# A decoder layer on one core: block 1's products with the expert input table made dense, the output columns split 768/256

## The chip, the core and the metric

The kernel runs on one core of a Trainium2 chip. The metric is the device time of one execution in microseconds. Before the change three runs took 1105.27, 1107.07 and 1106.55 us, so the median is 1106.55 us.

## What is computed

One decoder layer on 256 tokens of width 1024: a mixer (sparse attention beside gated linear attention), a cross-attention to a fixed memory, and PEER, a retrieval among 128 x 128 experts of one neuron each, with a layer norm behind each. The change lies in PEER alone:

```python
# 8 heads; per head the 16 best of 128 x 128 pairs of sub-keys: experts (T, 128), gates (T, 128)
def block(args):                       # one block of 128 tokens
    xt, et, gt = args
    u = expert_down[et]                # input table: 16384 rows of 1024
    act = jax.nn.gelu(jnp.einsum('td,tkd->tk', xt, u), approximate=False)
    vv = expert_up[et]                 # output table: 16384 rows of 1024
    return jnp.einsum('tk,tkd->td', gt * act, vv)
```

Every token so takes 128 rows of each table. There are two blocks of 128 tokens, called block 0 and block 1.

## The kernel before

TensorE (PE), VectorE (DVE), ScalarE (ACT) and GpSimd (POOL) are fed by Python code which is unrolled into one program. The framework orders each engine's instructions by priority and simulated readiness, starting from the order in which the code writes them; SP (SyncE) issues the plain loads and POOL the gathers.

**Up to about 269 us** the mixer, the cross-attention's keys and block 0's attention run. The change doesn't touch them.

**Input rows, 269 to 785 us.** `pick` (L645) finds the best keys and experts of one or two heads on DVE: `best16` (L748) with MAX8, FIND_INDEX8 and MATCH_REPLACE8, then one-hot products. `query` (L899) loads 1 MB of query weights and makes a head's scores on PE. `down` (L915) handles one column of 128 experts at a time: POOL gathers 128 rows of 4 KB, one for each token (`gd`, five buffers, L924 to L926), and DVE multiplies them with the tokens and sums (`junk`, L927), which gives one column of `wt`. There are 128 such steps for block 0 and 128 for block 1. For block 1 the tokens are first rearranged: `spread` (L711) and `quarter_rows` (L935) put each token on four partitions, so that a gather serves 32 tokens with four experts each.

The loop at L1050 mixes picks, rows and, from its step 5, the scatter. **The scatter** turns the gated weights of a block into a matrix `W[b]` of all 16384 experts against 128 tokens: `second_keys` (L1005) writes one-hot columns of the second sub-key with five ACT instructions for four tokens, and `weights` (L1014) makes for each token a one-hot of the first sub-key times the weights on DVE (`oa`, L1036), a product on PE of the strided column `W[b][:, :, t]` with it (L1037, two matmul instructions, as for each fp32 product), and writes back four tokens at a time on ACT (L1041). Block 1's scatter (L1116 to L1145) follows each quarter of its rows.

**Output table, 777 to 1084 us.** `up_dense` (L1166) loads the output table row by row (`u`, 128 pieces of 512 KB), splits each into a high and a low part (`uh` on ACT L1178, `ul` on DVE L1179), splits `W` alike (`w`, L1172 and L1173), and multiplies: three terms, each of them 512 columns per matmul into `py`. Block 0 has all 1024 columns by matmul, block 1 only the first `CD` = 512; its other 512 come from `up_rows_dve` (L1100), which gathers half rows (`gu`, L945) and sums them on DVE (`yq`, L1109). That makes 9 matmuls of 512 columns for a table row. A layer norm and the stores end the kernel (L1202 to L1226).

Of the kernel before, what the change touches and what calls it, by code (L numbers as in the profile page):

```python
# [44 lines left out]
OA = 6  # L45
YQ = 1
# [37 lines left out]
def kernel(ctx: ExitStack, tc, I, out):  # L84
# [560 lines left out]
    def pick(b, h0, n):  # L645

        def heads(t):

            if b == 0:
                return t[:, h0 * 16:(h0 + n) * 16].rearrange("p (n r) -> p n r", n=n)  # L650
            return t.rearrange("p (m g r) -> p m g r", m=4, g=2)[:, h0 % 4:h0 % 4 + n, h0 // 4, :]

        sel = [heads(PK[b]["sel"][:, e, :]) for e in range(2)]
        if b == 0:
            ei, gt = heads(PK[0]["ei"]), heads(PK[0]["gt"])
        else:
            ei, gt = heads(eg[:, 0, :]), heads(eg[:, 1, :])
# [42 lines left out]
        vec.scalar_tensor_tensor(ei[:, :, rs], sel[0][:, :, rs], 128.0, sel[1][:, :, rs], op0=OP.mult, op1=OP.add)  # L700
# [7 lines left out]
        if b == 1 and h0 + n in (4, 8):  # L708
            spread(h0 // 4)

    def spread(g):  # L711


        p = smt("sp").rearrange("p (q e r) -> p q e r", q=16, e=2)
        for q in range(4):
            for m in range(4):
                pe.matmul(p[32 * m:32 * m + 32, q], lhsT=ident[:, 32 * q:32 * q + 32],
                          rhs=eg[:, :, 32 * m + 16 * g:32 * m + 16 * g + 16],
                          start=True, stop=True, tile_position=(0, 32 * m))
        for e, nm in enumerate(("ei", "gt")):  # L720
            vec.tensor_copy(PK[1][nm].rearrange("p (q r) -> p q r", q=4)[:, :, 16 * g:16 * g + 16], p[:, :4, e, :])
# [45 lines left out]
    def picked(b):  # L767
        pt = smt("tp")
        for e in range(2):
            pe.transpose(pt[:, e * 128:(e + 1) * 128], PK[b]["sel"][:, e, :], ident)  # L770
        ixT = PK[b]["ixT"] = keep.tile([128, 128], FT, tag="ixT", name="ixT")
        nix = PK[b]["nix"] = keep.tile([128, 128], FT, tag="nix", name="nix")
        act.copy(ixT, pt[:, 0:128])
        act.mul(nix, pt[:, 128:256], -1.0)  # L774
# [100 lines left out]
    eg = work.tile([128, 2, 128], FT, tag="sc", name="eg", bufs=2)  # L875
# [37 lines left out]
    junk = consts.tile([128, DM], BF, name="junk")  # L913

    def down(b, pieces, tokens):  # L915

        ei, wt, gt = [PK[b][k] for k in ("ei", "wt", "gt")]
        xs = {}
        for i, j in enumerate(pieces):
            for k in range(16 * j, 16 * j + 16):  # L920
                for q in {0: pieces[i:i + 1], QR: pieces[i + 1:i + 2]}.get(k % 16, ()):
                    if q // 2 not in xs:
                        xs[q // 2] = tokens(q // 2)
                g = gath.tile([128, DM], FT, tag="gd", name="gd")  # L924
                gp.indirect_dma_start(out=g, out_offset=None, in_=I["dn"],  # L925
                                      in_offset=bass.IndirectOffsetOnAxis(ap=ei[:, k:k + 1], axis=0))  # L926
                vec.tensor_tensor_reduce(out=junk, in0=g, in1=xs[j // 2], scale=1.0, scalar=0.0, op0=OP.mult,  # L927
                                         op1=OP.add, accum_out=wt[:, k:k + 1])
                if k % 16 == 15:
                    hs = slice(k - 15, k + 1)  # L930
                    act.activation(wt[:, hs], wt[:, hs], AF.Gelu)
                    vec.tensor_mul(wt[:, hs], wt[:, hs], gt[:, hs])
                yield

    def quarter_rows(q, pool, tag, bufs, fold):  # L935

        x = pool.tile([128, DM], FT, tag=tag, name="xq", bufs=bufs)
        rs = slice(32 * q, 32 * q + 32)
        for i in range(2):
            p, cs = smt("xq"), slice(512 * i, 512 * i + 512)  # L940
            pe.matmul(p, lhsT=fold[rs, :], rhs=H2[1][rs, cs], start=True, stop=True, tile_position=(32 * q, 0))
            act.copy(x[:, cs], p)
        return x

    def up_row(b, k, pool):  # L945
        g = pool.tile([128, CG], FT, tag="gu", name="gu")
# [21 lines left out]
    def rest(b):  # L968
# [8 lines left out]
        if b == 0:  # L977
# [4 lines left out]
        h2T[b] = slot("h2T", [128, 8, 128])  # L982
# [4 lines left out]
    fold = load(work, "fold", [128, 128], tag="k4")  # L987
    rows = itertools.chain(down(0, range(8), lambda q: H2[0]),
                           down(1, (0, 2)[:EARLY], lambda q: quarter_rows(q, work, "pp", 3, fold)))
# [15 lines left out]
    def second_keys(b, g):  # L1005

        nix = PK[b]["nix"]
        o = W[b][:, :, 4 * g:4 * g + 4]
        for j in range(4):
            t = 4 * g + j  # L1010
            act.activation(o[:, :, j], iot, AF.Abs, bias=nix[:, t:t + 1])  # L1011
        act.activation(o, o, AF.Relu, scale=-1.0, bias=1.0)

    def weights(b):  # L1014
# [3 lines left out]
        if b == 0:  # L1018
            pt = smt("tr")
            pe.transpose(pt[:, 0:128], PK[b]["wt"], ident)  # L1020
            vec.tensor_copy(wT, pt[:, 0:128])
        ps = {}
        for g in range(33):
            if b == 1 and g % 8 == 0 and g < 32:
                pt, qs = smt("tr"), slice(4 * g, 4 * g + 32)
                for m in range(4):
                    ms = slice(32 * m, 32 * m + 32)
                    pe.matmul(pt[ms, 0:32], lhsT=PK[1]["wt"][ms, qs], rhs=ident[ms, ms], start=True, stop=True,
                              tile_position=(32 * m, 32 * m))
                vec.tensor_copy(wT[:, qs], pt[:, 0:32])  # L1030
            if g < 32:
                ps[g] = smt("wb")
                for j in range(4):
                    t = 4 * g + j
                    a = sml.tile([128, 128], FT, tag="oa", name="oa", bufs=OA)
                    vec.tensor_scalar(a, iot, ixT[:, t:t + 1], wT[:, t:t + 1], op0=OP.is_equal, op1=OP.mult)  # L1036
                    pe.matmul(ps[g][:, j * 128:(j + 1) * 128], lhsT=W[b][:, :, t], rhs=a, start=True, stop=True)  # L1037
                    yield
            if g:
                t0 = 4 * (g - 1)  # L1040
                act.activation(W[b][:, :, t0:t0 + 4], ps[g - 1].rearrange("p (j i) -> p i j", j=4), AF.Copy)  # L1041

    todo = ((0, 1, 2), (0, 3, 2), (0, 5, 2), (0, 7, 1), (1, 0, 2), (1, 2, 2), (1, 4, 2), (1, 6, 2))
    both = HB + 1
    asked = {0: [(h, (0,)) for h in range(QF, 3)], 1: [(h, (0,) if h <= HB else B2) for h in (3, 4)],
             2: [(h, B2) for h in (5, 6, 7)], 3: [(h, (1,)) for h in (1, 2)],
             4: [(h, (1,)) for h in (3, 4) if h <= HB]}
    nd, nk, nw = 0, 0, 0
# [239 lines left out]
```

## Time and profile before

| | |
|---|---|
| median of three runs | 1106.55 us |
| the profiled execution, its own time | 1103.19 us |
| its span, first to last instruction | 1101.1 us |
| busy: PE, DVE, ACT, POOL | 801.6, 941.1, 517.8, 494.9 us |
| moved by DMA | 293.39 MB, mean 266 GB/s |

The page gives an engine's busy time as a share of the span. A busy PE is modelled from pipelined instructions, so matmuls are better counted by their starts. [...]

### The profile page before, as it was taken

How to read it: one execution, taken by the hardware profiler on the slowest of the kernel's cores; microseconds unless marked ns; L12 is line 12 of the kernel's file. 1: busy time of each engine (PE TensorE's matmuls, PEld its weight loads, DVE VectorE, ACT ScalarE, POOL GpSimd, SP SyncE). 2: the span in 40 equal slices, each digit the busy share in tenths (PEclk: the TensorE clock that was granted, in tenths of full speed). 3: DMA queues.
4: the chain of work that ended last, by engine and by line, in shares of the span. 5: the costliest groups of instructions: out<-in, count | busy, mean ns of one | idle time of the engine just before them, and what ended most of it. 6: DMA issues, size and time to landing. Idle time of an engine off the chain costs nothing. (4 is left out here: it accounts for less than half of the span.)

```text
span 1101.1 us, 13910 instructions
## 1 busy us (share of the span) xinstructions
PE 801.6 (73%) x4341; PEld 653.2 (59%) x4341; DVE 941.1 (85%) x2155; ACT 517.8 (47%) x983; POOL 494.9 (45%) x391
## 2 busy tenths in 40 slices
PE   7999998997658910010556866853799999999994
PEld 6998878987548800000344545643677677677772
DVE  6957877556877899999997999999799998899996
ACT  5557653451202211896124894211255556565661
POOL 0000000001555786567533768787265662476671
PEclk9999999898779965555555655655799999999997
DMA  8454224554989988888864888788589999899993
GB/s 299 158 189 171 98 96 173 178 185 143 337 286 377 335 300 317 314 300 283 273 210 131 320 283 302 257 308 303 222 304 352 342 355 325 288 353 364 356 358 115
DMA packets 76297, 293.39 MB, mean 266 GB/s; under 512 B 9520, under 2 KB 10304, under 8 KB 70208
## 3 DMA queue, kind: packets, MB, share of 16 engines
q0 software_dynamic: 47104, 167.80, 43.7%
q1 hardware_dynamic: 28832, 123.67, 31.6%
q10 hardware_dynamic: 288, 1.05, 0.3%
q8 instruction: 34, 0.56, 0.2%
q14 instruction: 39, 0.32, 0.1%
HBM read 291.43 MB, written 1.05 MB: 266 GB/s over the span
## 5 line engine op out<-in xcount | busy, mean ns | idle before, releaser
L925 POOL DMA_INDIRECT gd<-dn,ei x256 | 314.8, 1230 | 433.4 <-ACT s1b L897 267.8
L947 POOL DMA_INDIRECT gu<-upg,ei x128 | 175.3, 1369 | 149.0 <-DVE yq L1109 77.2
L76 PE MATMUL py<-uh,w 128*128 128x512 f32 x768 | 222.1, 396 | 20.9 <-ACT uh L1178 19.5
L76 PE MATMUL wb<-oa,W 128*128 128x128 f32 x512 | 148.9, 444 | 74.1 <-DVE oa L1036 73.0
L1178 ACT ACTIVATE uh<-u 128x1024 fp32r<-128x1024 f32 x128 | 135.7, 1060 | 116.0 <-PE py L76 80.8
L76 PEld LDWEIGHTS wb<-oa,W 128*128 128x128 f32 x512 | 120.0, 308 | 111.3 <-DVE oa L1036 71.9
L76 PEld LDWEIGHTS py<-uh,w 128*128 128x128 f32 x768 | 145.1, 190 | 56.8 <-ACT uh L1178 20.4
L927 DVE CUSTOM_DVE_ANT_0 junk<-gd,h 128x1024 bf16<-128x1024 f32 x128 | 155.3, 1213 | 17.4 <-DMA gd<-dn,ei 16.7
L927 DVE CUSTOM_DVE_ANT_0 junk<-gd,xq 128x1024 bf16<-128x1024 f32 x128 | 155.6, 1215 | 10.7 <-DMA gd<-dn,ei 10.5
L1179 DVE TENSOR_TENSOR ul<-u,uh 128x1024 fp32r<-128x1024 f32 x128 | 156.0, 1219 | 9.7 <-ACT uh L1178 9.0
L76 PE MATMUL py<-ul,w 128*128 128x512 f32 x384 | 139.8, 418 | 5.2 <-DVE ul L1179 4.9
L239 DVE TENSOR_TENSOR wlo<-w,whi 128x1024 fp32r<-128x1024 f32 (+1 forms) x68 | 81.3, 1196 | 46.9 <-PE mm L76 35.7
L1109 DVE SCALAR_TENSOR_TENSOR yq<-gu,wt,yq 128x512 f32<-128x512 f32 x124 | 93.0, 750 | 6.2 <-DMA gu<-upg,ei 5.4
L237 ACT ACTIVATE whi<-w 128x1024 fp32r<-128x1024 f32 (+1 forms) x68 | 70.5, 1039 | 53.4 <-PE mm L76 39.8
L1041 ACT ACTIVATE W<-wb 128x512 f32<-128x512 f32 x64 | 38.1, 597 | 113.3 <-PE wb L76 113.2
L76 PEld LDWEIGHTS py<-ul,w 128*128 128x128 f32 x384 | 64.8, 190 | 44.0 <-DVE ul L1179 34.3
L1011 ACT ACTIVATE W<-ii,nix 128x128 f32<-128x128 f32 x256 | 89.1, 491 | 0.4 <-ACT nix L774 0.4
L1036 DVE TENSOR_SCALAR oa<-ii,ixT,wT 128x128 f32<-128x128 f32 x256 | 80.1, 347 | 5.5 <-PE wb L76 2.2
L76 PE MATMUL mm<-whi,xPh 128*128 128x256 f32 (+1 forms) x176 | 50.9, 292 | 6.1 <-ACT xPh L246 6.1
L76 PE MATMUL mm<-h2T,w 128*128 128x128 f32 x448 | 52.3, 275 | 2.8 <-DMA w<-pq 2.8
L76 PE MATMUL mm<-wlo,xPh 128*128 128x256 f32 (+1 forms) x176 | 52.0, 296 | 1.6 <-DVE wlo L239 1.6
L76 PEld LDWEIGHTS mm<-h2T,w 128*128 128x128 f32 x448 | 51.1, 192 | 3.5 <-DMA w<-pq 3.4
(332 smaller groups left out, 1398.3 us busy)
## 6 DMA issues: line engine op xcount, KB each, us to landing
u<-upd SPq DMA_DIRECT2D x128, 512.0 KB, 6.0
w<-pq SPq DMA_DIRECT2D x10, 1024.0 KB, 5.0
w<-xo SPq DMA_DIRECT2D x8, 1024.0 KB, 4.8
w<-xk SPq DMA_DIRECT2D x4, 1024.0 KB, 6.0
w<-xv SPq DMA_DIRECT2D x4, 1024.0 KB, 4.8
w<-wo SPq DMA_DIRECT2D x4, 1024.0 KB, 4.8
w<-xq SPq DMA_DIRECT2D x4, 1024.0 KB, 4.8
gd<-dn,ei POOLq DMA_INDIRECT x256, 5.8
```

The costliest lines, as they stand in the source:

```text
L76: self.eng.matmul(out, lhsT=lhsT, rhs=rhs, **kw)
L237: act.activation(hi, src, AF.Copy)
L239: eng.tensor_sub(lo, src, hi.bitcast(FT))
L925: gp.indirect_dma_start(out=g, out_offset=None, in_=I["dn"], in_offset=bass.IndirectOffsetOnAxis(ap=ei[:, k:k + 1], axis=0))
L927: vec.tensor_tensor_reduce(out=junk, in0=g, in1=xs[j // 2], scale=1.0, scalar=0.0, op0=OP.mult, op1=OP.add, accum_out=wt[:, k:k + 1])
L947: gp.indirect_dma_start(out=g, out_offset=None, in_=I["upg"], in_offset=bass.IndirectOffsetOnAxis(ap=PK[b]["ei"][:, k:k + 1], axis=0))
L1011: act.activation(o[:, :, j], iot, AF.Abs, bias=nix[:, t:t + 1])
L1036: vec.tensor_scalar(a, iot, ixT[:, t:t + 1], wT[:, t:t + 1], op0=OP.is_equal, op1=OP.mult)
L1041: act.activation(W[b][:, :, t0:t0 + 4], ps[g - 1].rearrange("p (j i) -> p i j", j=4), AF.Copy)
L1109: vec.scalar_tensor_tensor(y, g, wt[:, k:k + 1], y, op0=OP.mult, op1=OP.add)
L1178: act.activation(uh, u, AF.Copy)
L1179: (gp if i % LOW == LOW - 1 else vec).tensor_sub(ul, u, uh.bitcast(FT))
```

## The change

Block 1 gathers no input rows any more. The input table is handed over a second time, transposed (`dnT`: 128 pieces of 128 x 8 x 128, 512 KB each), and `dense` multiplies every piece with block 1's transposed tokens (8 products accumulated), four pieces to a PSUM bank; ACT writes gelu of it into `W[1]`. Only block 1's gates are scattered, into `W[0]`, and `gates` multiplies them in. Then block 0's weights are scattered into `W[0]`. 108 of the pieces are written beside block 0's gathers (steps 46 to 122), 20 beside block 0's scatter. `second_keys` goes: `equal` compares eight tokens at once on DVE in bf16, and ACT widens the result to fp32. In the last part block 0 now gathers 256 output columns and has 768 by matmul, block 1 has 1024 by matmul; the order of DVE, PE and ACT is the written one there, with the splits of a table row two rows ahead of its products.

```diff
-CD = 512
+CD = 768
+PICKS = ((4, 12), (14, 30), (30, 46), (46, 54), (54, 60), (60, 66), (66, 72), (72, 78))
+ROOM, CHANGE = 3, 78
+SCAT1 = (80, 116)
+DENSE = 27
+DPACE = (46, 122)
+AHEAD = 2
...
+    def dense():
+        for g in range(32):
+            ps = smt("sc")
+            for m in range(4):
+                d = ust.tile([128, 8, 128], FT, tag="uh", name="d", bufs=3)
+                nc.sync.dma_start(out=d, in_=I["dnT"][4 * g + m])
+                for c in range(8):
+                    pe.matmul(ps[:, m * 128:(m + 1) * 128], lhsT=d[:, c, :], rhs=h2T[1][:, c, :], start=(c == 0),
+                              stop=(c == 7))
+                if m < 3:
+                    yield
+            ps = ps.rearrange("p (i t) -> p i t", i=4)
+            o = W[1][:, 4 * g:4 * g + 4, :]
+            if g < DENSE:
+                act.activation(o, ps, AF.Gelu)
+            else:
+                a = sml.tile([128, 4, 128], FT, tag="eq", name="ge", bufs=2)
+                act.activation(a, ps, AF.Gelu)
+                vec.tensor_mul(o, o, a)
+            yield
...
+    def equal(b, t0):
+        eq = sml.tile([128, 128, 8], BF, tag="eq", name="eq", bufs=2)
+        vec.tensor_tensor(eq, iot8, PK[b]["ix2"][:, None, t0:t0 + 8].to_broadcast([128, 128, 8]), op=OP.is_equal)
+        return eq
...
+                if g % 2 == 0:
+                    o2 = ul_pool.tile([128, 128, 8], FT, tag="ul", name="o2", bufs=3)
+                    act.activation(o2, equal(b, 4 * g), AF.Copy)
...
-                    pe.matmul(ps[g][:, j * 128:(j + 1) * 128], lhsT=W[b][:, :, t], rhs=a, start=True, stop=True)
+                    pe.matmul(ps[g][:, j * 128:(j + 1) * 128], lhsT=o2[:, :, t % 8], rhs=a, start=True, stop=True)
...
+    def gates():
+        for g in range(32):
+            o, w = [W[b][:, 4 * g:4 * g + 4, :] for b in (1, 0)]
+            if g < DENSE:
+                vec.tensor_mul(o, o, w)
+            else:
+                act.copy(o, w)
+            yield
...
+    for now in range(128):
...
+        take(rows, 1)
+        if 1 in W:
+            pace("dn", gd, 4 * DENSE, DPACE)
+        if 0 in W:
+            pace("w1", gw[1], 133, SCAT1)
+    drain(gw[1], gates())
+    rest_d = 128 - 4 * DENSE
+    for k in range(128):
+        take(gw[0], 1)
+        while at["dn"] < 4 * DENSE + rest_d * (k + 1) // 128:
+            take(gd, 1)
+            at["dn"] += 1
...
+    parts0 = ((py[0][0], halves[0]), (py[0][1][:, 0:CD - 512], slice(512, CD)))
+    parts1 = tuple(zip(py[1], halves))
...
+            for p, cs in (parts0, parts1)[b]:
+                pe.matmul(p, lhsT=l[:, i % 4, :], rhs=r[:, cs], start=False, stop=(last and n == 2 and p is not parts0[1][0]))
...
+    with tc.manual_schedule(engines={mybir.EngineType.DVE, mybir.EngineType.PE, mybir.EngineType.Activation}):
+        for s in range(AHEAD):
+            part_row(s)
+        for s in range(128):
+            for b in B2:
+                up_products(b, s, *us[s], s == 127)
+            if s + AHEAD < 128:
+                part_row(s + AHEAD)
+            take(gr, 1)
+        drain(gr)
...
+    a["dnT"] = A(a["dn"].reshape(128, 128, 8, 128).transpose(0, 3, 2, 1))
```

`W[1]` and the buffers of `d` are placed where the query weights lay (at step 46), `W[0]` where the picks' tiles lay (at step 78).

## Rows read from the trace of the kernel before

**Rows 1.** The page: busy time of each engine, and the clock by slices.

```profile
PE 801.6 (73%) x4341; PEld 653.2 (59%) x4341; DVE 941.1 (85%) x2155; ACT 517.8 (47%) x983; POOL 494.9 (45%) x391
PEclk9999999898779965555555655655799999999997
```

**Rows 2.** Busy time by stretch: length, PE, PEld, DVE, ACT, POOL, clock, DMA share, GB/s.

```profile
269.00:375.00 106.00, 77.92 (x543) 72.10 (x542) 87.92 (x279) 18.53 (x51) 60.44 (x48) 0.87 0.92 335
340.00:375.00 35.00, 30.98 (x274) 30.59 (x273) 31.56 (x105) 8.09 (x21) 19.20 (x15) 1.00 0.98 380
800.00:1075.00 275.00, 270.68 (x1110) 199.90 (x1109) 258.46 (x299) 163.89 (x184) 161.61 (x116) 0.99 0.96 341
269.00:785.00 516.00, 261.05 (x1223) 203.58 (x1221) 469.25 (x1348) 204.69 (x525) 325.15 (x266) 0.61 0.85 294
```

**Rows 3.** Groups of instructions by line: busy us, mean ns; idle before.

```profile
L1179 DVE TENSOR_TENSOR ul<-u,uh 128x1024 fp32r<-128x1024 f32 x128 | 156.0, 1219 | 9.7 <-ACT uh L1178 9.0
L927 DVE CUSTOM_DVE_ANT_0 junk<-gd,h 128x1024 bf16<-128x1024 f32 x128 | 155.3, 1213 | 17.4 <-DMA gd<-dn,ei 16.7
L1109 DVE SCALAR_TENSOR_TENSOR yq<-gu,wt,yq 128x512 f32<-128x512 f32 x124 | 93.0, 750 | 6.2 <-DMA gu<-upg,ei 5.4
L1011 ACT ACTIVATE W<-ii,nix 128x128 f32<-128x128 f32 x256 | 89.1, 491 | 0.4 <-ACT nix L774 0.4
L1173 DVE TENSOR_TENSOR w<-W,w 128x512 fp32r<-128x512 f32 x64 | 43.8, 685 | 2.5 <-ACT w L1172 1.5
```

**Rows 4.** Last stage, PE in order of time: the first matmuls of three table rows.

```profile
930.32 0.74 PE L76 MATMUL py<-ul,w 128*128 128x512 f32 x2
...
932.53 0.62 PE L76 MATMUL py<-ul,w 128*128 128x512 f32 x2
...
934.64 0.73 PE L76 MATMUL py<-ul,w 128*128 128x512 f32 x2
```

**Rows 5.** Instructions reducing gathered rows (tile `junk`) from 269 to 375 us.

```profile
269.00:375.00 106.00, 54.42 (x45) 0.87 0.92 335
```

**Rows 6.** The last instruction of each pick (L707) in the same stretch.

```profile
269.00:375.00 106.00, 0.52 (x3) 0.87 0.92 335
```

**Rows 7.** In order of time: fp32 products with contiguous weights; the scatter's products and one-hots.

```profile
351.11 7.31 PE L76 MATMUL mm<-h2T,w 128*128 128x128 f32 x64
...
782.25 5.27 DVE L1036 TENSOR_SCALAR oa<-ii,ixT,wT 128x128 f32<-128x128 f32 x15
...
787.21 10.15 PE L76 MATMUL wb<-oa,W 128*128 128x128 f32 x46
```

**Rows 8.** DVE in order of time: two-input bf16 operations, 512 elements, in pairs.

```profile
501.20 1.28 DVE L689 TENSOR_TENSOR oh<-abf,iob 128x512 bf16<-128x512 bf16 x2
502.41 0.77 DVE L694 TENSOR_TENSOR oh<-oh,i16f 128x512 bf16<-128x512 bf16 x2
```

**Rows 9.** In order of time, PE: 256-column matmuls back to back, first and 27th.

```profile
204.79 0.28 PE L76 MATMUL mm<-hPh,wlo 128*128 128x256 f32 x1
...
207.91 0.28 PE L76 MATMUL mm<-hPh,wlo 128*128 128x256 f32 x1
```

**Rows 10.** DMA issues: count, KB each, median us from issue to landing.

```profile
u<-upd SPq DMA_DIRECT2D x128, 512.0 KB, 6.0
...
x<-x SPq DMA_DIRECT2D x2, 512.0 KB, 7.5
```

**Rows 11.** The end: last matmul of the last stage.

```profile
1084.58 0.39 PE L76 MATMUL py<-uh,w 128*128 128x512 f32 x1
```

**Rows 12.** PE in stretches of 5 us: busy time, clock, DMA share, GB/s.

```profile
345.00:350.00 5.00, 2.16 (x20) 1.00 1.01 410
...
650.00:655.00 5.00, 3.22 (x11) 0.50 0.89 311
...
780.00:785.00 5.00, 5.00 (x26) 0.74 1.03 404
785.00:790.00 5.00, 5.00 (x25) 1.00 0.28 107
```

More of the change, by code (lines that the diff above doesn't have):

```diff
@@ L911, in query @@
             key_products(b, h, pqT[:, :, TS[b]])
[L913 to L933, printed above, removed]
@@ L985, in rest @@
         yield
-    fold = load(work, "fold", [128, 128], tag="k4")
-    rows = itertools.chain(down(0, range(8), lambda q: H2[0]),
-                           down(1, (0, 2)[:EARLY], lambda q: quarter_rows(q, work, "pp", 3, fold)))
+    rows = down()
     iob = small.tile([128, 16], BF, tag="iob", name="iob", bufs=1)
@@ L1017, in weights @@
         wT = sml.tile([128, 128], FT, tag="wT", name="wT", bufs=2)
[L1018 to L1021, printed above, removed]
+        pt = smt("tr")
+        pe.transpose(pt[:, 0:128], PK[b]["gt" if b else "wt"], ident)
+        vec.tensor_copy(wT, pt[:, 0:128])
         ps = {}
         for g in range(33):
[L1024 to L1030, printed above, removed]
@@ new lines, with pace, make_room @@
+    at = {}
+    now = 0
+    def pace(name, gen, n, span, most=None):
+        want = min(n, -(-n * (now + 1 - span[0]) // (span[1] - span[0])))
+        while at.get(name, 0) < (want if most is None else min(want, most)):
+            next(gen, None)
+            at[name] = at.get(name, 0) + 1
+    gw = [weights(b) for b in B2]
+    gd = dense()
+    ust = sml = iot8 = None
+    def make_room():
+        nonlocal sml, ust, iot8
+        ctxL.close()
+        big = ctxB.enter_context(tc.tile_pool(name="big1", bufs=1))
+        ust = ctxB.enter_context(tc.tile_pool(name="ust", bufs=2))
+        sml = ctxB.enter_context(tc.tile_pool(name="sml", bufs=2))
+        W[1] = big.tile([128, 128, 128], FT, name="W1")
+        iot8 = big.tile([128, 128, 8], BF, name="iot8")
+        act.copy(iot8, iot[:, :, None].to_broadcast([128, 128, 8]))
@@ L1054 @@
             query(*q)
-        if i == 5:
-            ctxL.close()
+        if i == ROOM:
+            make_room()
+        gpick[i] = pick(*todo[i])
+    halves = slice(0, 512), slice(512, DM)
+    for now in range(128):
+        for i, span in enumerate(PICKS):
+            if now >= span[0]:
+                if i not in gpick:
+                    begin(i)
+                n = 18 if todo[i][2] == 2 else 12
+                pace(("pick", i), gpick[i], n, span)
+                if i == 0:
+                    take(other, 1)
+                if now >= span[1] - 1 and at.get(("picked", i)) is None:
+                    at["picked", i] = 1
+                    drain(gpick[i])
+                    if i == 3:
+                        picked(0)
+                    if i == 7:
+                        picked(1)
+        if now == CHANGE:
+            ctxP.close()
+            wp = ctxB.enter_context(tc.tile_pool(name="wp", bufs=2))
+            h2T[1], h = wp.tile([128, 8, 128], FT, tag="w", name="h2T"), h2T[1]
+            act.copy(h2T[1], h)
+            ctxA.close()
@@ L1057 @@
             big = ctxB.enter_context(tc.tile_pool(name="big0", bufs=1))
[L1058 removed]
+            ul_pool = ctxB.enter_context(tc.tile_pool(name="ulp", bufs=3))
+            sml2 = ctxB.enter_context(tc.tile_pool(name="sml2", bufs=2))
             W[0] = big.tile([128, 128, 128], FT, name="W0")
[L1060 to L1065 removed]
@@ L1066 @@
-        steps = 18 if n == 2 else 12
-        d0 = nd
-        for j, _ in enumerate(pick(b, h, n)):
-            take(other, i < HB // 2 and j % OM == 0)
-            while nd < min(ready, d0 + -(-DR[i] * (j + 1) // steps)):
-                take(rows, 1)
-                nd += 1
-            if i >= 5:
-                while nk < min(32, K0[i - 5] * (j + 1) // steps + sum(K0[:i - 5])):
-                    take(gk0, 1)
-                    nk += 1
-                while nw < min(4 * nk, WE[1] * (nd - 128 - WE[0])):
-                    take(gw, 1)
-                    nw += 1
```

226 lines of the change are left out of this document (64 added, 162 removed).

## The prediction, made before the change was run

> **What bounds the kernel now.** I read the page first. No engine is full over the whole span (DVE 85%, PE 73%), and the clock falls to half in the middle [rows 1], so there are stages with different limits. The table by stretch gives them. From 269 to 785 us, where rows are gathered, DVE is busy 469 of 516 us and PE 261 [rows 2]: DVE ends that stage. In its first 106 us DVE has 88 and DMA is at 0.92, so there the two are close [rows 2]. From 800 to 1075 us PE shows 271 of 275 us, but that is modelled time and misleads. The rows by line tell: a table row costs DVE 1.219 (`ul`), half of a group of four's two `w`, 0.34, and 0.750 (`yq`) [rows 3], together 2.31 us, and 128 such rows are 296 us. PE alone needs less: where no gather disturbs it, two table rows, 18 matmuls, take 934.64 - 930.32 = 4.32 us, 2.16 a row or 0.240 us for one matmul of 512 columns [rows 4]. So DVE bounds both long stages, and behind the last matmul at 1084.6 us [rows 11] comes a tail of 16.5 us that the change leaves alone.
>
> **Steps 0 to 45.** Before, 45 reductions and 3 picks (five heads) were done by 375 us [rows 5, 6]. Now step 46 also wants `pick`'s next two heads done. The 8 DVE calls before handled 16 heads; DVE's 469 us less 256 reductions of about 1.24 us (1.213 and the start of the next) [rows 3] and less some 230 one-hots of 0.351 us (5.27 / 15) [rows 7] leave about 70 us, some 4 us a head. Of two heads, 8 us, a part hides in DVE's 18 us of gaps [rows 2], so step 46 comes at 380 us (375 to 383).
>
> **Steps 46 to 127.** What goes: block 1's 128 reductions with their gathers, about 159 us of DVE, the rearranged tokens and `second_keys` with 256 ACT instructions, 89 us [rows 3], which were beside other work. What comes is costed on each resource, and the slowest sets the end.
> - DVE: 82 reductions x 1.24 = 102; nine heads x 4 = 36; block 1's scatter 128 x 0.351 = 45 [rows 7]; 16 `equal` of 1024 bf16 elements. That last isn't in the trace; twice the 512-element rows are 0.77 or 1.28 us [rows 8]. Its inner operand is contiguous as in the faster one, so 0.77, 12 us in all (20 at the other end). Sum 195 us.
> - PE: a product of 128 x 128 x 128 in fp32 takes two instructions, 2 x 7.31 / 64 = 0.228 us [rows 7]. A piece is 8, 1.83 us; 108 pieces are 197 us. The scatter's 128 products add 29 to 56 (below). Sum 226 to 253 us.
> - DMA: 82 gathers and 108 pieces of 0.524 MB are 99.6 MB. The trace sustained 380 GB/s (340 to 375 us, gathers beside loads), 341 in the last stage and 335 at 0.92 share [rows 2]: 262, 292 or 297 us. I take 355 GB/s, the middle, as the mix is nearer to the first row but runs eight times as long: 281 us.
> DMA sets the end, at 380 + 281 = 661 us. SP waits for a free `d` before each load; behind it stand only loads of later pieces and then `u`, whose first use comes after both scatters, so that wait delays no one else.
>
> **Between.** `gates` is 27 products of 128x512 on DVE, 0.685 us like `w` [rows 3], 18 us; DVE has 86 us to spare above, and only the last groups must wait for the last pieces: 6 us (0 to 18). Block 1's scatter matrix must be used up before block 0's overwrites it. Last gather, gelu, transpose and the first one-hot: 4 us, estimated from the small steps of that chain.
>
> **Block 0's scatter.** Before, three quarters of it lay beside block 1's gathers; now it stands alone on the path, as nothing of it can start before the last reduction. DVE: 128 x 0.351 + 16 x 0.77 = 57 us. PE: 20 pieces x 1.83 = 37, of which some 5 fit into the 10 us before, so 27; and 128 products. The old ones cost 2 x 10.15 / 46 = 0.441 us where PE was their bound, against 0.228 with contiguous weights [rows 7]: their stationary operand steps by 512 bytes. The new one steps by 32, nearer to contiguous (4) than to 512, so I take 0.228, 29 us. PE's sum is 56, DVE's 57, and they hand over token by token through four buffers: 65 us. With 0.441 it is 27 + 56 + 7 = 90.
> [...]
>
> **Last stage.** PE now has, for a table row, 9 matmuls of 512 columns and 3 of 256. The latter follow each other in (207.91 - 204.79) / 26 = 0.120 us [rows 9]. 9 x 0.240 + 3 x 0.120 = 2.52 us; 128 rows are 323. DVE drops to 1.219 + 0.34 + `yq` of 256, between 0.375 and 0.750, so at most 2.31: PE becomes the bound, and the two rows of lead cover ACT and DVE. The 0.240 holds some hand-overs which the lead of two rows should remove, so I take 320 (315 to 332), 3 us to start, and the tail of 16.5.
>
> **Sum.** 380 + 281 + 6 + 4 + 65 + 3 + 320 + 16.5 = 1075.5 us of span, 25.6 below the 1101.1 of the profiled span. That execution's own time was 1103.19 us, 3.4 below the median of 1106.55; taken off the median this gives 1081 us. Less than 0.2%, about 2 us, can't be told from no change here.
>
> **The rivals.**
> - *Three buffers are too few (slower).* A piece holds its `d` from issue to its last product. With a landing of 6.0 us, as `u` has under a full DMA [rows 10], a piece comes every (6.0 + 1.83) / 3 = 2.61 us, and 108 take 282 us: just the bandwidth's figure. With 7.5 us, as `x` had [rows 10], it is 3.11 us and 336 us, 55 more: 1136 us. It decides from a landing of about 6.8 us, where the 26 us are gone. For it: the gathers' queue has five buffers and takes its share first. Against it: loads with little in flight land sooner. Chance 0.14.
> - *PE stays at half clock.* Pieces are bursts of 1.8 us, and in the old scatter, 3.2 us busy in 5, the clock was 0.50 [rows 12]. [...] Against it: a PE that slow would be the bound and never idle, and 5.00 busy at 780 raised the clock to 1.00 [rows 12]; once there, 2.16 of 5 us kept it at 345 [rows 12]. Chance 0.06.
> [...]
> - *The last stage takes back the gain (no change).* If every matmul pays more than its steady price, say 0.26 for 512 columns where DVE hands over late, 128 rows cost 350: about 1107 us. For it: a row has 12 hand-overs of weights in place of 9, and DVE's order is now fixed, so a late gather holds up the next `ul`. Against it: DVE's slack and the lead. Chance 0.08.
> - *The change doesn't do what it says: block 1's gates aren't scattered beside the gathers.* `W[0]` lies where the picks' tiles lay, so the scatter can't start before the last pick; if picks slip behind step 116, all of it, 128 x 0.441 = 56 us, falls behind the last gather: 1137 us. Against it: DVE has 86 us to spare. Chance 0.06.
>
> **How the numbers follow.** The forecast has 0.66. Its own range: all low ends (375, 262, 0, 57, 315) take off 5 + 19 + 6 + 8 + 5 = 43, 1038 us; the high ends of DMA (297), scatter and last stage add 16 + 25 + 12 = 53, 1134. From 1038 to 1130 the range so takes in the third rival and milder cases of the first and fourth, and leaves out the half clock and all the worst ends at once. Faster: 0.63 of the forecast's 0.66 (its high ends aside) and 0.02 each of the first and third rival, 0.67. Same: 0.06 of the third. Slower: 0.12 of the first, 0.06 of the second, 0.06 of the fourth and 0.03 of the forecast, 0.27.
>
> **What would show it.** Right: `dense` matmuls every 2.6 us on average between 380 and 661 us at a clock of 1.00, DMA share above 0.95, DVE under 80% busy there; scatter products at 0.23 us; the last stage at 2.5 us a row with DVE under 90%. Wrong: a DMA share near 0.8 with SP waiting for PE (three buffers); a clock of 0.50 there; products of 0.44 us in block 0's scatter; DVE ending the last stage's waits.

## The result, and the profile after

The changed kernel takes 1147.26 us (median of 4 runs, 1140.27 to 1151.46) where the kernel before takes 1106.46 in the same comparison: a ratio of 1.036 (1.030 to 1.042). The forecast was 1081, so the sign was wrong and the time lies above the range. The profiled execution has a span of 1148.9 us and took 1150.64.

The page of the changed kernel: busy time, the granted TensorE clock in 40 slices (tenths of full speed), and the chain that ended last, by engine and by line (answers to [rows 1]).

```profile
PE 1025.4 (89%) x6648; PEld 941.2 (82%) x6648; DVE 812.7 (71%) x1944; ACT 448.3 (39%) x712; POOL 284.3 (25%) x263
PEclk9999998998888899899999999999999999999997
PE 73%; DMA 15%; DVE 6%; ACT 3%; issue 2%; POOL 1%; SPq 0%; ACTq 0%; DVEq 0%; POOLq 0%
PE py L74 28%; PE mm L74 16%; PE sc L74 15%; DMA d<-dnT 11%; PE wb L74 10%; DMA gd<-dn,ei 2%; PE tp L78 1%; DMA w<-xo 1%; DVE wlo L237 1%; DVE gd L899 1%; PE go L74 1%; ACT whi L235 1%; PE ks L74 1%; POOL gd L897 1%; PE xo L74 1%
```

The change did to the engines what it said: DVE falls from 941 to 813 us, POOL from 495 to 284, and the clock no longer sinks to half in the middle. But PE rises by 224 us, and the chain that ended last is PE's for 73%, with a tenth of the whole span in `wb`, the scatter products. So the bound moved to PE and to the loads that PE waits for. Where: busy time by stretch, columns as in [rows 2]. The stretches are the steps before the first dense product, the first 143 us of the dense work, the stretch with block 1's scatter added, the rest of block 1 after the last gathers, block 0's scatter, and the last stage.

```profile
269.00:390.00 121.00, 88.56 (x620) 82.71 (x618) 100.74 (x354) 24.07 (x67) 64.23 (x51) 0.87 0.86 306
397.00:540.00 143.00, 107.20 (x796) 100.23 (x796) 99.72 (x378) 32.18 (x65) 46.18 (x42) 0.93 0.90 325
540.00:628.00 88.00, 83.88 (x574) 82.54 (x575) 69.78 (x154) 22.01 (x34) 37.81 (x34) 1.00 0.98 376
628.00:718.00 90.00, 88.42 (x637) 87.06 (x638) 44.57 (x102) 23.88 (x37) 0.00 (x0) 1.00 0.68 225
718.00:816.00 98.00, 94.66 (x553) 94.20 (x553) 50.88 (x138) 33.42 (x48) 0.64 (x1) 0.98 0.27 94
820.00:1130.00 310.00, 309.41 (x1518) 258.50 (x1519) 241.71 (x319) 166.63 (x189) 123.86 (x125) 1.00 0.86 265
```

Two different things are seen. From 397 to 540 us no column is full: PE has 107 of 143, DVE 100, DMA 0.90. From 540 us on PE is busy 95 to 100% of every stretch. Up to 628 us DMA is full beside it (0.98); then it falls to 0.68 and 0.27, and transfers no longer set the end. The prediction had DMA as the bound up to 661 us.

The groups of instructions that belong to it: busy us, mean ns, then idle time before them and what ended it (answers to [rows 3, 7]).

```profile
L74 PE MATMUL sc<-h2T,d 128*128 128x128 f32 x2048 | 258.7, 284 | 48.3 <-DMA d<-dnT 48.2
L74 PEld LDWEIGHTS sc<-h2T,d 128*128 128x128 f32 x2048 | 247.7, 199 | 56.3 <-DMA d<-dnT 36.5
L1010 DVE TENSOR_SCALAR oa<-ii,ixT,wT 128x128 f32<-128x128 f32 x256 | 87.2, 350 | 83.2 <-PE wb L74 62.1
L74 PE MATMUL wb<-oa,o 128*128 128x128 f32 x512 | 132.3, 403 | 4.2 <-ACT o L1006 3.3
L74 PEld LDWEIGHTS wb<-oa,o 128*128 128x128 f32 x512 | 126.6, 333 | 5.1 <-ACT o L1006 3.7
```

The dense products (`sc`) and the scatter products (`wb`) have the same shape, 128 x 128 x 128 in fp32. A dense one loads its weights in 199 ns as a mean, a scatter one in 333, and DVE's one-hots wait 62 us for PE, not PE for DVE. In order of time, PE, in block 0's scatter:

```profile
745.47 3.02 PE L74 MATMUL wb<-oa,o 128*128 128x128 f32 x12
748.32 1.95 PE L74 MATMUL sc<-h2T,d 128*128 128x128 f32 x16
750.11 2.06 PE L74 MATMUL wb<-oa,o 128*128 128x128 f32 x8
```

Two instructions are one product (2048 of `sc` for 128 pieces of 8). The length of a run (3.02, 1.95 us) has a modelled end that reaches into the next run, so I read prices from start to start: six scatter products take 748.32 - 745.47 = 2.85 us, 0.475 each; eight dense ones 750.11 - 748.32 = 1.79 us, 0.224 each. The prediction took 0.228 for the scatter product and 0.441 as its worst; 256 of them at 0.475 are 122 us where 58 were counted.

The other thing is in the chain of waits, here from 396 to 460 us (start, us, what; its first eleven pieces), and in the DMA issues between 400 and 540 us (count, KB each, median us to landing), and SP's waits in the same stretch (us in all, times, longest).

```profile
389.29 7.47 DMA d<-dnT
396.76 0.14 issue
396.90 3.51 PE sc L74 x16
400.41 0.02 issue
400.43 6.58 DMA d<-dnT
407.01 0.04 issue
407.05 7.14 PE sc L74 x48
414.20 0.02 issue
414.21 5.85 DMA d<-dnT
420.07 0.04 issue
420.11 2.06 PE sc L74 x16
```

```profile
d<-dnT SPq DMA_DIRECT2D x49, 512.0 KB, 6.4
gd<-dn,ei POOLq DMA_INDIRECT x40, 7.5
```

```profile
SPq L913 <- PE sc L74: 94.5, 47, 5.5
```

A load of `d` starts 0.02 us after a product has given a buffer back, lands 6 us later, and then its own product runs: in this chain products and loads take turns. SP waits 47 times for PE. With three buffers a piece can come every (6.4 + 2.0) / 3 = 2.8 us, 2.0 being the products of a piece. Of the 796 instructions in the 143 us up to 540, 784 are dense products: 49 pieces, 2.92 us a piece.

So the miss by stage, from the first and last starts of three groups (first load of `d`; the last of `gates`, L1021; first and last product into `py`):

```profile
L913 SPq DMA_DIRECT2D d<-dnT x128: 327/328/426, 389.3 to 803.9; - x128
L1021 DVE TENSOR_TENSOR W<-W,W x27: 682/683/692, 697.4 to 715.6; 128x512 f32<-128x512 f32 x27
L74 PE MATMUL py<-uh,w x1024: 277/394/501, 819.3 to 1133.3; 128*128 128x512 f32 x171
L74 PE MATMUL py<-yq,ii x2: 377/378/378, 1133.5 to 1133.7; 128*128 128x256 f32 x2
```

| stage | forecast | measured | miss |
|---|---|---|---|
| step 46 (first `d` issued) | 380 | 389.3 | +9 |
| dense work up to the end of `gates` | 281 + 6 = 287 | 716.3 - 389.3 = 327 | +40 |
| last-gather chain, block 0's scatter, start of the last stage | 4 + 65 + 3 = 72 | 819.3 - 716.3 = 103 | +31 |
| last stage | 320 | 1134.1 - 819.3 = 314.8 | -5 |
| tail | 16.5 | 1148.9 - 1134.1 = 14.8 | -2 |
| span | 1075.5 | 1148.9 | +73 |

### The profile page after: what moved, and what is told of

The parts are those of the page before. It is cut to its first block, busy times and chain, and to the rows that moved or that the text cites. A ratio compares the mean times of both kernels' runs of the same rounds, so it can differ in the third digit from the quotient of the medians.

```text
span 1148.9 us, 17834 instructions
## 1 busy us (share of the span) xinstructions
PE 1025.4 (89%) x6648; PEld 941.2 (82%) x6648; DVE 812.7 (71%) x1944; ACT 448.3 (39%) x712; POOL 284.3 (25%) x263
## 3 DMA queue, kind: packets, MB, share of 16 engines
q10 hardware_dynamic: 288, 1.05, 0.2%
HBM read 274.52 MB, written 1.05 MB: 240 GB/s over the span
## 4 chain that ended last, share of the span: by engine, by line
PE 73%; DMA 15%; DVE 6%; ACT 3%; issue 2%; POOL 1%; SPq 0%; ACTq 0%; DVEq 0%; POOLq 0%
PE py L74 28%; PE mm L74 16%; PE sc L74 15%; DMA d<-dnT 11%; PE wb L74 10%; DMA gd<-dn,ei 2%; PE tp L78 1%; DMA w<-xo 1%; DVE wlo L237 1%; DVE gd L899 1%; PE go L74 1%; ACT whi L235 1%; PE ks L74 1%; POOL gd L897 1%; PE xo L74 1%
## 5 line engine op out<-in xcount | busy, mean ns | idle before, releaser
L74 PE MATMUL sc<-h2T,d 128*128 128x128 f32 x2048 | 258.7, 284 | 48.3 <-DMA d<-dnT 48.2
L74 PEld LDWEIGHTS sc<-h2T,d 128*128 128x128 f32 x2048 | 247.7, 199 | 56.3 <-DMA d<-dnT 36.5
L897 POOL DMA_INDIRECT gd<-dn,ei x128 | 152.0, 1187 | 469.2 <-ACT s1b L875 267.6
L74 PE MATMUL py<-uh,w 128*128 128x512 f32 (+1 forms) x1024 | 250.8, 367 | 1.0 <-ACT uh L1153 1.0
L931 POOL DMA_INDIRECT gu<-upg,ei x128 | 127.6, 997 | 375.4 <-PE wb L74 193.3
L899 DVE CUSTOM_DVE_ANT_0 gd<-gd,h 128x1024 f32<-128x1024 f32 x128 | 154.3, 1214 | 22.5 <-DMA gd<-dn,ei 22.3
L74 PE MATMUL py<-ul,w 128*128 128x512 f32 (+1 forms) x512 | 145.5, 366 | 0.6 <-DVE ul L1154 0.6
L74 PE MATMUL wb<-oa,o 128*128 128x128 f32 x512 | 132.3, 403 | 4.2 <-ACT o L1006 3.3
L74 PEld LDWEIGHTS wb<-oa,o 128*128 128x128 f32 x512 | 126.6, 333 | 5.1 <-ACT o L1006 3.7
L1122 DVE SCALAR_TENSOR_TENSOR yq<-gu,wt,yq 128x256 f32<-128x256 f32 x127 | 60.6, 477 | 0.1
```

The costliest lines, as they stand in the source:

```text
L74: self.eng.matmul(out, lhsT=lhsT, rhs=rhs, **kw)
L897: gp.indirect_dma_start(out=g, out_offset=None, in_=I["dn"], in_offset=bass.IndirectOffsetOnAxis(ap=ei[:, k:k + 1], axis=0))
L899: vec.tensor_tensor_reduce(out=g, in0=g, in1=H2[0], scale=1.0, scalar=0.0, op0=OP.mult, op1=OP.add, accum_out=wt[:, k:k + 1])
L1122: vec.scalar_tensor_tensor(y, g, wt[:, k:k + 1], y, op0=OP.mult, op1=OP.add)
```

## The experiments

Two theories came out of this. **A:** the load of the strided stationary operand makes the scatter product dear, and PE the bound. **B:** the dense work is held by its loads through three buffers. All edits below are made to the changed kernel. Some kernels have a single time; the runs of one kernel here differ by up to 1.2% from their median, so single times are read to 10 us and finer readings rest on rows.

**e1_contig, e2_noload, e3_contig_noload: each cause taken out, and both.**

```diff
-                    o2 = ul_pool.tile([128, 128, 8], FT, tag="ul", name="o2", bufs=3)
-                    act.activation(o2, equal(b, 4 * g), AF.Copy)
+                    o2 = ul_pool.tile([128, 8, 128], FT, tag="ul", name="o2", bufs=3)
+                    act.activation(o2.rearrange("p t i -> p i t"), equal(b, 4 * g), AF.Copy)
...
-                    pe.matmul(ps[g][:, j * 128:(j + 1) * 128], lhsT=o2[:, :, t % 8], rhs=a, start=True, stop=True)
+                    pe.matmul(ps[g][:, j * 128:(j + 1) * 128], lhsT=o2[:, t % 8, :], rhs=a, start=True, stop=True)
```

> Only the layout of the spread second keys changes: ACT writes them as [128, 8, 128], so that a scatter product loads its stationary operand from neighbouring columns in place of columns 32 bytes apart. Theory A (the strided load makes a scatter product cost 0.52 us, and PE sets the end from 545 us on): a product falls to about 0.24 us; block 0's scatter, 103 us from the last product of block 1 to the last stage, falls to about 70, the dense stretch loses up to 30 more, 1085 to 1105 us. Rival B (the dense stretch is set by transfers through three buffers): the product gets cheaper all the same, but only block 0's scatter gains, about 30 us: 1117 us. Rival C (the product's price is the hand-over of a new one-hot and a new PSUM place, not the layout): 0.5 us stays, 1147 us.

e2_noload:

```diff
-                d = ust.tile([128, 8, 128], FT, tag="uh", name="d", bufs=3)
-                nc.sync.dma_start(out=d, in_=I["dnT"][4 * g + m])
+                if g == 0 and m == 0:
+                    d = ust.tile([128, 8, 128], FT, tag="uh", name="d", bufs=3)
+                    nc.sync.dma_start(out=d, in_=I["dnT"][0])
```

> All 128 dense pieces multiply the first piece of the table, which is loaded once; the other 127 loads are left out, with the layout of the second keys as it was. Theory A: up to about 540 us PE loses its waits for loads, at most 38 us; from there on PE was full already, so 1110 to 1125 us. Rival B: the whole dense stretch, 325 us long, shrinks to DVE's or PE's sum, 250 us at most, so below 1080 us.

> Both edits at once: contiguous second keys, and one load for all dense pieces (the products are all made, with the first piece of the table). Theory A: PE's sum for the dense stretch is 108 x 1.94 + 128 x 0.24 = 240 us, and block 0's scatter is 65 to 70 us: about 1040 us, clearly below the two edits' gains added where each was masked by the other. Rival B: as with the one load alone, less some 30 us in block 0's scatter.

Measured: 1106.21 us (1098.28 to 1113.71, 10 runs; ratio to the kernel before 0.998, 0.995 to 1.001) for the layout alone, 1102.99 for the loads alone, 1044.80 for both. The groups of e1_contig:

```profile
L74 PE MATMUL sc<-h2T,d 128*128 128x128 f32 x2048 | 263.7, 287 | 57.5 <-DMA d<-dnT 55.4
L74 PE MATMUL wb<-oa,o 128*128 128x128 f32 x512 | 70.7, 282 | 8.2 <-ACT o L1006 7.1
L74 PEld LDWEIGHTS wb<-oa,o 128*128 128x128 f32 x512 | 64.7, 194 | 9.5 <-ACT o L1006 7.7
```

The same loads of the same size take 194 ns in place of 333, and PE's busy time for the scatter falls from 132.3 to 70.7 us. Rival C (hand-over sets the price) is out. Of these 62 us of PE only 41 came off the time: PE's waits for `d` rose from 48 to 55 us, those for `o`, which ACT now writes in 2.0 us a group, from 3 to 7, and of the chain that ended last loads of `d` were 75% between 540 and 628 us, where they had been 35%. With the loads left out alone 44 us went, more than theory A allowed (38) and less than B wanted (67). Both together took 102 us, 17 more than the two alone (41 + 44): A's figure of about 1040 held, and each cost had been hiding behind the other.

**e7_step8 and e11_step16: what step of the columns costs.** The prediction had argued that a step of 32 bytes lies nearer to 4 than to 512.

```diff
-                    o2 = ul_pool.tile([128, 128, 8], FT, tag="ul", name="o2", bufs=3)
+                    o2 = ul_pool.tile([128, 4, 128, 2], FT, tag="ul", name="o2", bufs=3)
...
-                    pe.matmul(ps[g][:, j * 128:(j + 1) * 128], lhsT=o2[:, :, t % 8], rhs=a, start=True, stop=True)
+                    pe.matmul(ps[g][:, j * 128:(j + 1) * 128], lhsT=o2[:, t % 8 // 2, :, t % 2], rhs=a, start=True, stop=True)
```

(ACT writes it through the same view; e11_step16 is [128, 2, 128, 4].)

> The changed kernel with the spread second keys as [128, 4, 128, 2]: a product's stationary columns lie 8 bytes apart, in place of 32 (changed kernel) or 4 (e1_contig). If the price grows with the step, as my prediction took it, the load lies nearer to 192 ns than to 335, and the time at 1110 to 1120 us. If any step over the element's own size costs the whole of it, the load takes 335 ns and the time is that of the changed kernel, 1140 to 1150 us.

> The changed kernel with the spread second keys as [128, 2, 128, 4]: a product's stationary columns lie 16 bytes apart. e7_step8 gave 196 ns a load at 8 bytes, the changed kernel 335 at 32. If the price is a threshold above 16 bytes: 192 to 200 ns and 1100 to 1110 us. If the price grows between 8 and 32 with the bytes: 240 to 290 ns and 1115 to 1135 us. If the threshold is below 16: 335 ns and 1140 to 1150 us.

Measured: 1103.98 us and 1150.20 us. The weight loads of the scatter products, min/median/max in ns, first of e7_step8, then of e11_step16:

```profile
L74 PEld LDWEIGHTS wb<-oa,o x512: 192/196/333, 544.8 to 772.8; 128*128 128x128 f32 x171
```

```profile
L74 PEld LDWEIGHTS wb<-oa,o x512: 308/329/332, 547.6 to 815.5; 128*128 128x128 f32 x171
```

The same of the changed kernel, at a step of 32 bytes, and of e1_contig, at 4:

```profile
L74 PEld LDWEIGHTS wb<-oa,o x512: 312/335/340, 547.9 to 816.0; 128*128 128x128 f32 x171
```

```profile
L74 PEld LDWEIGHTS wb<-oa,o x512: 186/192/333, 543.7 to 773.5; 128*128 128x128 f32 x171
```

In the kernel before, at a step of 512 bytes:

```profile
L76 PEld LDWEIGHTS wb<-oa,W x512: 291/312/316, 529.1 to 796.9; 128*128 128x128 f32 x171
```

| step between columns | 4 bytes | 8 | 16 | 32 | 512 (kernel before) |
|---|---|---|---|---|---|
| median load, ns | 192 | 196 | 329 | 335 | 312 |

Of these five steps the jump lies between 8 and 16 bytes, and there is no slope: a load takes 4 ns more at 8 than at 4, and 137 more at 16. (e7_step8's time fell below both of its expectations; e11_step16 came out as its third.) The kernel before ran its loads at both levels of the clock, and the median was 313 ns from 640 to 660 us, at 0.50, as from 786 to 797, at 1.00. So the prediction's interpolation by bytes falls. What makes the jump is not shown.

**e4_fourbufs: a fourth buffer for `d`, at the gathers' cost**, in e1_contig's kernel.

```diff
-    gath = ctx.enter_context(tc.tile_pool(name="gath", bufs=5))
+    gath = ctx.enter_context(tc.tile_pool(name="gath", bufs=4))
...
-                d = ust.tile([128, 8, 128], FT, tag="uh", name="d", bufs=3)
+                d = ust.tile([128, 8, 128], FT, tag="uh", name="d", bufs=4)
...
```

> Contiguous second keys as in e1_contig, and four buffers in place of three for the dense pieces (the last stage's uh shares them), paid for with four in place of five for the gathered rows. Theory B1 (what is left of the dense stretch, 55 us of PE waiting for d, comes from the hand-back of a buffer to the load after it, while DMA has room): the waits fall to 25 us or less, 1075 to 1085 us. Theory B2 (DMA itself is full there, at 0.82 to 0.96 of its time and 303 to 367 GB/s): PE's waits stay near 50 us, and DVE waits longer for the gathers, which now have four in flight, 1105 to 1115 us.

Measured: 1095.77 us, between the two expectations. PE's waits for `d` did fall, from 55 to 24 us, and DMA went from 0.90 and 328 GB/s (e1_contig) to 0.98 and 378 between 390 and 540 us: DMA had room, B1. But the gathers with four buffers run from the start of the block, and the first `d` was issued at 400.8 us, not 388.4, while DVE's waits for rows rose from 27 to 47 us.

**e5_half and e10_half_strided: block 0's last part undone**, with and without the new layout.

```diff
-CD = 768
+CD = 512
...
-    parts0 = ((py[0][0], halves[0]), (py[0][1][:, 0:CD - 512], slice(512, CD)))
+    parts0 = ((py[0][0], halves[0]),)
...
```

(Beside this, the one-hots of four tokens share one tile in both kernels, in two buffers, to make room.)

> Contiguous second keys as in e1_contig, and block 0's last part undone: 512 columns dense and 512 gathered, with the pipelined order of the last stage kept. (The gathered rows alternate between two pools, two buffers each, for room.) Theory L1: PE bounds the last stage of the changed kernel with 12 matmuls a row, 312 us for 128 rows; with 8 a row it falls back to the 2.25 us a row of the kernel before, 288 us, where DVE and DMA are the bound: 1106 - 24 = 1082 us. Rival L2: DVE's order is fixed by hand now, so that every late gather (512 columns again) holds up the next subtraction, and the row stays at 2.4 us or more: 1105 to 1115 us.

> The changed kernel with its last part alone undone (512 columns gathered for block 0, pipelined order kept); the second keys stay 32 bytes apart. The gain of e5_half over e1_contig, 27 us by the profiled spans and 34 by the medians, lies in the last stage and should not depend on the layout: 1113 to 1121 us. If it does depend on it (the scatter hides what the last stage saves), less than 15 us is gained: above 1132 us.

Measured: 1072.58 us (ratio 0.968, 0.966 to 0.970) and 1115.84 us. The last stage of e5_half, as stretch:

```profile
781.00:1060.00 279.00, 270.52 (x1149) 214.00 (x1149) 270.03 (x319) 165.20 (x190) 205.29 (x126) 0.99 0.97 355
```

L1 holds, but with 9 matmuls a row, not the 8 of the expectation (1152 for 128 rows, the 9 of the kernel before): PE (270.5 of 279), DVE (270.0) and DMA (0.97) are all close to full, and the stage takes 280 us where 12 matmuls take 312 with PE at 100% and DVE at 78%. With the keys 32 bytes apart it is 281 us (e10_half_strided) against 315. The 256 columns that block 0 does not gather any more cost 32 us, whatever the layout is.

**e6_half_fourbufs: e4_fourbufs and e5_half together.**

> Both edits of e4_fourbufs and e5_half. B1 with L1: about 1055 us, as they lie in different stages and add. B2 with L1: about 1085 us. B1 with L2: 1080 us.

Measured: 1078.68 us; they did not add. The last stage began at 773.2 us, 7 before e5_half's, but took 6 us longer: `u` had four buffers as well, and ACT's wait for `u` rose from 11 to 88 us.

**e8_share4 and e9_share2: more room for `d` out of the gathers' pool**, each fourth or second piece.

```diff
-                d = ust.tile([128, 8, 128], FT, tag="uh", name="d", bufs=3)
+                d = (gath.tile([128, 8, 128], FT, tag="gd", name="d") if m == 3 else
+                     ust.tile([128, 8, 128], FT, tag="uh", name="d", bufs=3))
```

> e5_half with more buffers for the dense pieces at no cost in room: each fourth piece takes one of the gathered rows' five buffers, the others the three of before. Theory B1 (hand-back of buffers holds the loads): PE's waits for d fall from 57 us to about 25, and step 46 comes no later than in e5_half, unlike in e6_half_fourbufs: 1045 to 1060 us. Theory B2: a gather now waits behind a dense piece's products for its buffer, DVE waits longer for rows, and the steps stretch by what PE gains: 1070 to 1085 us.

> As e8_share4, but every second piece takes one of the gathered rows' buffers. B1: PE's waits for d fall below 25 us, 1040 to 1055 us. B2: gathers wait still longer, 1080 us or more.

Measured: 1099.06 and 1099.29 us, both some 26 us slower than e5_half: B2, and in e8_share4 beyond its range. A pool hands its buffers out in turn, so gathers and dense pieces now wait for each other. Between 395 and 640 us of e8_share4, SP's loads of `d` waited 99 us for DVE, which they never did in e5_half, and POOL's gathers 9 us for PE; how much of the loss each makes is not shown. DVE's waits for rows in e8_share4:

```profile
DVE gd L899 <- DMA gd<-dn,ei: 80.6, 33, 6.5
```

They were 10.4 us in e5_half over the same stretch (395 to 640 us).

**e12_half_step8, e13_fifth, e14_own_order.** e12 is e5_half with the keys 8 bytes apart; e13 adds the fourth buffer only from the start of the dense pieces: the fifth gather buffer lies beside the query weights and ends with them, and from then on its room holds a fourth `d`, and in the last stage a fifth `u`; e14 takes the written order out of e12.

```diff
-    gath = ctx.enter_context(tc.tile_pool(name="gath", bufs=5))
+    gath = ctx.enter_context(tc.tile_pool(name="gath", bufs=4))
+    fifth = dict(n=0, pool=ctxL.enter_context(tc.tile_pool(name="fifth", bufs=1)), tag="gx")
+    def gtile(shape, dt, name):
+        fifth["n"] += 1
+        if fifth["n"] % 5 == 0 and fifth["pool"] is not None:
+            return fifth["pool"].tile(shape, dt, tag=fifth["tag"], name=name, bufs=1)
+        return gath.tile(shape, dt, tag="gd", name=name)
...
         ctxL.close()
+        fifth["pool"] = None
...
-                d = ust.tile([128, 8, 128], FT, tag="uh", name="d", bufs=3)
+                d = ust.tile([128, 8, 128], FT, tag="gx" if m == 3 else "uh", name="d", bufs=1 if m == 3 else 3)
...
+    fifth.update(n=0, pool=ust)
```

And of e14_own_order, against e12_half_step8:

```diff
-    with tc.manual_schedule(engines={mybir.EngineType.DVE, mybir.EngineType.PE, mybir.EngineType.Activation}):
+    if True:
```

> e5_half with the second keys 8 bytes apart in place of 4, where ACT spreads a group in 1.12 us and not in 2.00 and a product costs the same. PE no longer waits some 7 us for the spread keys in block 0's scatter; it is the bound there, so the time falls by 0 to 7 us: 1065 to 1073 us.

> e12_half_step8 with a fourth buffer for the dense pieces from their start on, taken from the gathered rows' five only then (five stay up to the third pick's end, and u has five again in the last stage). e6_half_fourbufs, which took it for the whole run, came to its first dense product 14 us later and to its last stage 7 us earlier, and lost that again in the last stage. Theory B1 (the hand-back of three buffers holds the loads): the dense stretch is 15 to 22 us shorter than in e12_half_step8, 1045 to 1058 us. Rival B2 (with four buffers for the gathers, as much is lost there in waits for rows): within 5 us of e12_half_step8.

> e12_half_step8 with the last stage's order left to the scheduler, as in the kernel before, and the two rows of lead in program order only. If the written-out order is what starts the last stage 1.3 us after the last scatter product, where the kernel before took some 20 us: a start of 15 to 20 us and 1085 to 1092 us. If the lead in program order does it by itself: within 3 us of e12_half_step8.

Measured: 1069.93 us (ratio 0.964, 0.959 to 0.970), 1046.00 and 1075.75. e13_fifth confirms B1. From 390 to 540 us, e12_half_step8 and then e13_fifth:

```profile
390.00:540.00 150.00, 113.28 (x812) 106.67 (x813) 104.47 (x393) 32.77 (x68) 51.70 (x45) 0.89 0.93 333
390.00:540.00 150.00, 124.87 (x971) 115.67 (x972) 123.26 (x445) 41.16 (x80) 53.64 (x53) 0.96 1.01 395
```

DMA is full at 395 GB/s with the same gathers and loads that ran at 333 through three buffers, and the last stage began at 750.3 us, not 768.2. The gathers paid for it: DVE's waits for rows rose from 11 to 33 us between 395 and 640 us. e14_own_order still began its last stage right behind the last scatter product (774.0 and 775.8 us) and took 281 us for it, e12's 280: the lead of two rows in program order does that, not the written order. The 6 us by which its time is above e12's are no more than runs of e12 differ.

**e16_fourth_only, e17_fourth_step8, e18_final: how the miss divides.** The fourth buffer of e13_fifth put into the changed kernel alone; the same with the keys 8 bytes apart; and e13_fifth run again.

> The changed kernel with the fourth buffer for the dense pieces alone (as in e13_fifth, five for the gathers up to the third pick's end); second keys 32 bytes apart, 256 columns gathered. PE was full from 545 us on in the changed kernel, so that only what PE waited for loads before can come back, 38 us less what DVE now waits longer for rows: 1112 to 1130 us. If the strided load were the only cause of the miss, nothing comes back: 1140 to 1150 us.

> The changed kernel with both suspected costs taken out, the load of the second keys (8 bytes apart) and the third buffer's hand-back (four buffers), and its last part as the change has it. This is what my forecast described; its sum gave 1081 us. With e13_fifth's 1046 and the 24 to 32 us that the last part costs more with 256 gathered columns: 1068 to 1080 us.

> e13_fifth again, to time it: second keys 8 bytes apart, four buffers for the dense pieces from their start on, 512 columns dense and 512 gathered for block 0. It was 1046 us in one look: 1040 to 1052 us, a ratio of 0.94 to 0.95 to the kernel before.

Measured: 1127.87 us; 1075.87 us (1075.04 to 1079.31, ratio 0.974, 0.971 to 0.978); 1049.51 us (1043.12 to 1054.41, ratio 0.948, 0.944 to 0.952). All three as expected.

| the change, in us | three buffers | four buffers |
|---|---|---|
| keys 32 bytes apart | 1147.3 | 1127.9 |
| keys 8 bytes apart | 1104.0 | 1075.9 |

The layout is worth 43 to 52 us, the fourth buffer 19 to 28, both 71. The 9 us that 43 and 19 leave open would be what each had hidden of the other, but two of the four times are single, and 9 us is no more than such times differ by. e18_final beats both kernels; beside the two repairs it undoes the last part (e17 against e18: 26 us).

## Why the prediction was wrong

**The step that failed** is the scatter product: "The new one steps by 32, nearer to contiguous (4) than to 512, so I take 0.228". It measured 0.475 us, above even the upper end of 0.441. The old product [rows 7] was the nearer row, its load 312 ns at 512 bytes, and I set it aside by measuring distance in bytes; e7_step8 and e11_step16 show that there is no slope to interpolate on. The term appears twice. In block 0's scatter 128 x (0.475 - 0.228) = 32 us are the whole miss of that stage (103 us for 72). In "Sum 226 to 253 us" the measured prices give 108 x 8 x 0.224 + 128 x 0.475 = 254 us, still under the 281 of the transfers; but PE also stood idle for 36 of the 143 us up to 540, mostly waiting for loads, and had that work left over. So "DMA sets the end, at 380 + 281 = 661 us" failed: from 540 to 628 us PE and DMA are both close to full (0.95 and 0.98), and from 628 us on PE alone is.

**"Three buffers are too few" was a rival and was in part what happened.** Its formula was right: (6.4 + 2.0) / 3 = 2.8 us a piece, 2.92 measured. I gave it 0.14 on the argument that a landing must reach 6.8 us to matter. For it I had the gathers: from 397 to 540 us DVE waited 3.9 us for their rows, PE 42 us for `d`. Against it I had that loads with little in flight land sooner: `d` did in 3.2 us from 718 to 816 us, at a DMA share of 0.27, but in 6.4 at 0.90. But the 355 GB/s that the rival was compared with was itself passed with one buffer more: 384 in e17_fourth_step8 and 395 in e13_fifth. Measured against 384, where 99.6 MB are 2.40 us for each of 108 pieces, three buffers bind already from a landing of 5.4 us, as (5.4 + 1.83) / 3 = 2.41; the landing was 6.4. Taken alone, its price was 19 to 28 us.

**The rest of the frame held.** With the two costs out, the change is what the sum described. Stretches and starts of e17_fourth_step8, first the stretches:

```profile
397.00:540.00 143.00, 118.62 (x929) 110.33 (x928) 117.41 (x422) 39.11 (x75) 52.88 (x48) 0.98 0.99 384
540.00:628.00 88.00, 75.44 (x627) 74.49 (x626) 60.84 (x147) 25.90 (x39) 27.68 (x25) 0.96 0.95 356
628.00:718.00 90.00, 86.20 (x747) 85.39 (x746) 54.79 (x151) 35.91 (x54) 0.00 (x0) 1.00 0.58 200
```

```profile
L920 SPq DMA_DIRECT2D d<-dnT x128: 327/328/655, 383.3 to 730.6; - x128
L1028 DVE TENSOR_TENSOR W<-W,W x27: 684/685/693, 656.5 to 672.8; 128x512 f32<-128x512 f32 x27
L74 PE MATMUL py<-uh,w x1024: 277/389/504, 747.1 to 1057.7; 128*128 128x512 f32 x171
```

Step 46 at 383.3 (380 forecast), the end of `gates` at 673.5 (667), the last stage from 747.1 (739), 1075.9 us in all against 1081. One point of it came out by luck: DMA is the bound only up to 628 us; the last 45 us before `gates` end are PE's, because the dense pieces run behind the gathers (the last row is reduced at 608 us) and block 1's scatter stands between them. Nor could `gates` run beside the scatter, as its 6 us had it: each of its products takes `W[0]` for all tokens, so 26 of the 27 ran in a row from 656.5 to 672.3 us, behind the scatter's last write. PE's last dense pieces ended at 672 as well.

**Point by point.** *Steps 0 to 45:* the first `d` was issued at 389.3 us, outside 375 to 383 (383 to 390 in e1_contig, e5_half, e12_half_step8, e16_fourth_only and e17_fourth_step8, where these steps are the same). The two heads cost their 8 us or more in full: DVE's gaps are 20 us of 121 now and were 18 of 106 before, so nothing of them hid there. The first product stood another 7.5 us behind its load, which the sum did not have. *DVE's terms* held: one-hot 0.350 us (0.351), `equal` 0.685 (0.77), `gates` 0.683 (0.685), `yq` 0.477 (0.375 to 0.750). A dense piece took 1.79 us from start to start (1.83). *Half clock:* wrong; the granted clock was 0.93 between 397 and 540 us and 1.00 from 540 to 718, though PE had bursts of 2 us between loads. It did fall to 0.50 for short stretches, as from 407 to 410 us behind a wait of PE of 3.1 us; there the median load of 128 neighbouring columns took 333 ns in place of 192, while the old scatter's loads took 313 ns at both levels. What the whole of the dense work would take at 0.50, no run shows. *Gates behind the last gather:* in part they did fall there, for PE's sake and not for the picks': when the last row was reduced at 633 us, 148 of the 256 matmuls of block 1's scatter had been made; the others took until 697, and `gates` ended at 716. *The last stage* was right in mechanism and size: 314.8 / 128 = 2.46 us a row for 2.50, PE at 100%, DVE at 78%. That this gives time away against 512 gathered columns stood in the sum (323 against 296 before), and e5_half shows that it is a loss by itself, of 32 us.

## What to carry to other kernels

Look at how far apart the columns of a stationary operand lie, before counting its products: of fp32, up to 8 bytes cost next to nothing here (a load of 196 ns for 192), and 32 bytes cost 0.25 us for every product of 128 x 128 x 128 (0.475 for 0.224), while the compare or copy that writes the operand can lay it out at almost no price (e7_step8: ACT 1.12 us a group for 1.05). A rate of transfer read from a trace belongs to the number of buffers that it was read with (333 GB/s with three here, 395 with four); price a loop of loads both by (landing + use) / buffers and by the rate, and take the longer time. And when two costs can each be the bound, one repair shows only part of its worth: undo both before judging either.

## What the runs showed that I had not expected

- The load of 128 fp32 columns: 192 ns at a step of 4 bytes, 196 at 8, 329 at 16, 335 at 32 and 312 at 512, with nothing between.
- ACT pays for the same layout question when it writes: a group of 1024 elements took 1.05 us at neighbouring places (changed kernel), 1.12 with pairs of neighbours (e7_step8) and 1.99 with places 512 bytes apart (e1_contig).
- Giving a producer more buffers out of a pool that another queue takes in turn made things worse by 26 us (e8_share4), where a buffer of its own brought 20 (e18_final against e12_half_step8).
